# A two-block transformer kernel: order of the first modulation, packed attention scores and values, gates by pair, and fp32 one-hots in the expert selection

## The chip, the core and the metric

One core of a Trainium2 chip runs the whole program. The metric is the device time of one execution in microseconds (us), the median of several runs. The core has TensorE for matrix products (PE in the rows; PEld is its loading of the stationary operand), VectorE (DVE), ScalarE (ACT), GpSimd (POOL) and SyncE (SP, which issues most DMAs). Each engine takes its instructions in order.

## What is computed

One sequence of 512 tokens with 1024 features passes through two blocks. The first has two layers, retention and forgetting attention, each under a modulation by a vector `c`; the second has stick-breaking attention beside a gated delta rule, and then a layer that selects 16 experts for each token and head out of 16384. What matters here:

```python
c_act = jax.nn.silu(c)
shift, scale, gate = jnp.split(c_act @ mod_w[i] + mod_b[i], 3, axis=-1)
h = _rms_norm(x, norm_g[i]) * (1.0 + scale[:, None, :]) + shift[:, None, :]
...
# forgetting attention: 16 heads of 64, blocks of 128 query rows
logits = (jnp.einsum('bhqd,bhkd->bhqk', q[:, :, qs:qe], k[:, :, :qe])
          + cum[:, :, qs:qe, None] - cum[:, :, None, :qe])
p = jax.nn.softmax(jnp.where(causal, logits, -jnp.inf), axis=-1)
outs.append(jnp.einsum('bhqk,bhkd->bhqd', p, v[:, :, :qe]))
...
return (o.astype(h.dtype) * jax.nn.silu(g)) @ w_out
...
# expert selection
cand = (v1[..., :, None] + v2[..., None, :]).reshape(B, S, PEER_HEADS, PEER_TOPK * PEER_TOPK)
vals, c = lax.top_k(cand, PEER_TOPK)
expert = e1 * PEER_N_KEYS + e2
gate = jax.nn.softmax(vals, axis=-1)
```

The whole is held to float32 accuracy. The kernel gets it from TensorE by splitting each operand into a rounded part (type float32r, "hi") and the rest ("lo"), and by taking hi·hi + hi·lo + lo·hi: three matrix products where one is meant (`mm3`, L213 to L215).

## The kernel before

A tile framework schedules the program: it orders each engine's instructions by its own plan, so that work of later steps stands between the work of earlier ones, and adds the semaphores. Where the code wants an order, it adds a dependency by hand (`add_manual_dep`, without a semaphore).

**Weights.** `weights` loads a 512 KB block into `wraw` (SP's queue, L203), rounds it on ACT (`whi`, L206) and takes the rest on DVE (`wlo`, L207). Three buffers of each.

**The start (`retention`, first part).** x is loaded, then the 8 blocks of modulation part 1 (scale) into the space of `hTh` and `hTl`, and the 8 of part 0 (shift) into that of `vh`, `vl`, `yh`, `yl`. `mod_first` makes one part: of the blocks named in `direct` the product with c goes to TensorE directly (8 small products each, L630); the others are summed on DVE (L642, then L645 with a running sum in `wlo`), and the sum goes to TensorE with 8 small products. `mod_part` adds the bias (L595). Of part 1 the blocks 4 to 7 are direct, of part 0 the blocks 0 and 1. A small product leaves two records in the trace. L505 brings the norm's factor R, L728 multiplies x by it (8 times), L738 to L740 make the layer's input `hTh`, `hTl`, and `pair` (L553) multiplies it by the first two weight blocks.

**Forgetting attention (`fox`).** Eight pairs of heads. `part_a(p)` projects q and k of a pair, normalizes them (`normed`) and transposes them into a PSUM bank "norm"; `values(g)` makes the values of two pairs, `gates(g)` the gates of two pairs, all with the three products. `part_b(h, g)` makes the scores of two blocks of 128 rows, i = 2g and 2g + 1, with n = 128(i + 1) columns: q and k of one head are 64 rows of the pair's tiles, so that the three products (L213 to L215) have 64 rows; then `pick` adds the forget sums `ncr` (L915, 128 rows), and a bf16 product the mask (L916). DVE takes the maximum (L918), ACT the exponential, and the probabilities are rounded to `ph`, their rest to `pl` (L925), both transposed (L933, L940) into `pt`. `part_c` multiplies them by the values (L957): three products for each key block, with stationary operands of the hi or the lo of both heads of the pair, of which one head's 64 rows of the result are used; L970 multiplies them by the gate. Score banks "mx" are three, transposes have one bank "tr", the result one, "po".

**Expert selection (`peer`).** In the stretch that makes the gate table, 96 groups of 4 tokens each take four one-hot rows times the gate (L1660, DVE: a bf16 `iob` of 0 to 127 compared with one pointer scalar and multiplied by another, written as float32), one bf16 comparison (L1662), a copy on ACT (L1664), and 4 products on TensorE (L1641). Meanwhile weight blocks of the next step are split, with their lo part on GpSimd (`self.lo`, L207 on POOL).

Of the kernel before, what the change touches and what calls it, by code (L numbers as in the profile page):

```python
# [140 lines left out]
class Kern:  # L141
# [4 lines left out]
    def __init__(self, tc, ctx, A, out):  # L146
        self.tc, self.nc, self.A, self.out = tc, tc.nc, A, out
        self.cst = self.pool(ctx, "cst")
        self.wp = self.pool(ctx, "wp", 3)
        self.sm = self.pool(ctx, "sm", 2)  # L150
        self.run = (None, [], None)
        self.bk = {}
        self.bs = ExitStack()
        self.banks(self.bs, side="right", acc=2, norm=1)
        self.bg = None
        self.lo = tc.nc.vector
        self.pre = None
        self.mods = {}
# [39 lines left out]
    def weights(self, src, shape, raw=None):  # L198
        if self.bg is not None:
            self.bg = self.bg if next(self.bg, 0) is None else None  # L200
        if raw is None:
            raw = self.wp.tile([128, 1024], F32, name="wraw")
        self.nc.sync.dma_start(raw, src)  # L203
        hi = self.wp.tile([128, 1024], F32R, name="whi")
        lo = self.wp.tile([128, 1024], F32R, name="wlo")
        self.nc.scalar.activation(hi, raw, AF.Copy)  # L206
# [54 lines left out]
    def normed(self, pool, ps, d, gains, out):  # L261
# [19 lines left out]
        for w in range(2):  # L281
            ps = self.ps("norm", (128, 4, 128))
            for t in range(4):
                nc.tensor.transpose(ps[:, t], raws[t // 2][:, t % 2, 128 * w:128 * w + 128], self.ident)
            hi, lo = out[w]
            p2 = ps.rearrange("p a b -> p (a b)")
            nc.scalar.activation(hi, p2, AF.Copy, scale=gains[:, w:w + 1])
            nc.vector.scalar_tensor_tensor(lo, p2, gains[:, w:w + 1], hi.bitcast(F32), op0=OP.mult, op1=OP.subtract)
# [28 lines left out]
    def narrow(self, pool, tag, src):  # L317

        nc = self.nc
        fr = pool.tile([128, 8, 16], F32, name="fr")  # L320
        nc.sync.dma_start(fr, src)
        fh = pool.tile([128, 8, 16], F32R, name="fh")
        fl = pool.tile([128, 8, 16], F32R, name="fl")
# [267 lines left out]
    def mod_part(self, part, ps, md, bias, g, a1):  # L591
# [3 lines left out]
        nc.vector.tensor_add(md[:, s], ps[:, :, 0], bias[:, s])  # L595
# [23 lines left out]
    def mod_first(self, part, ws, acc, tag, tiles, direct):  # L619
# [17 lines left out]
        begun = False  # L637
        for k in range(8):
# [5 lines left out]
            else:  # L644
                nc.vector.scalar_tensor_tensor(acc, ws[k], self.cact[:, k:k + 1], acc, op0=OP.mult, op1=OP.add)  # L645
            yield
        products(acc, self.ones2, True)
        self.mod_part(part, ps, *tiles)
# [39 lines left out]
    def retention(self):  # L688
        nc, A = self.nc, self.A
        off = (0, 512, 896, 1152)  # L690
        with ExitStack() as cx:
# [25 lines left out]
            v = small[:, 0:4]  # L717
            nc.vector.tensor_scalar(v, ss[:, :, 0], 1.0 / D, EPS, op0=OP.mult, op1=OP.add)
# [14 lines left out]
            self.pre = [self.weights(A["ret_qk"][0, i], (8, 128)) for i in range(2)]  # L733
            mod = self.mod(0, mp, "norm", tiles, (2,))
            self.hT = [self.cst.tile([128, 8, T], F32R, name=n) for n in ("hTh", "hTl")]
            for k in range(8):
                hi, lo = self.hT[0][:, k], self.hT[1][:, k]
                nc.scalar.activation(hi, ts[k], AF.Identity, bias=b0[:, k:k + 1], scale=a0[:, k:k + 1])  # L738
                nc.vector.tensor_scalar(ts[k], ts[k], a0[:, k:k + 1], b0[:, k:k + 1], op0=OP.mult, op1=OP.add)
                nc.vector.tensor_sub(lo, ts[k], hi.bitcast(F32))  # L740
            QK, V, PR, SG, Y = {}, {}, {}, {}, {}
# [100 lines left out]
    def fox(self):  # L842
# [3 lines left out]
        with ExitStack() as cx:  # L846
            self.banks(cx, mx=3, tr=1, po=1)
# [4 lines left out]
            ncr = self.rows_pair(pool, "ncr", 1)[0]  # L852
            ncum = pool.tile([128, 4, 16], F32, name="ncum")

            def forget():
# [11 lines left out]
                ones = pool.tile([128, 8, 16], F32, name="fr").rearrange("p a b -> p (a b)")  # L867
# [9 lines left out]
                self.split_rows(ncr, ps, 16)  # L877
# [3 lines left out]
            def part_a(p):  # L881

                ps = self.pair_wide() if self.pre else self.proj_wide(A["fox_qk"][p], self.hT)
                for w in range(2):
                    QK[p, w] = [pool.tile([128, T], F32R, name=f"qk{w}" + "hl"[z], bufs=2) for z in range(2)]
                self.normed(pool, ps, 64, gains, [QK[p, w] for w in range(2)])

            def values(g):

                pv = self.proj_wide(A["fox_v"][g], self.hT)  # L890
                for a in range(2):
                    v = V[2 * g + a] = [pool.tile([128, 4, 128], F32R, name="fv" + "hl"[z], bufs=3) for z in range(2)]
                    for t in range(2):
                        ts = slice(2 * t, 2 * t + 2)
                        self.split(v[0][:, ts], v[1][:, ts], pv[t][:, :, a * 128:a * 128 + 128])

            def gates(g):
                sg = SG[g] = pool.tile([128, 2, T], F32, name="fsg")
                for m in range(2):
                    pg = self.proj_cols(A["fox_g"][2 * g + m], self.hT)  # L900
                    self.act(sg[:, m], pg, AF.Silu)

            def part_b(h, g):

                p, e = divmod(h, 2)
                (qh, ql), (kh, kl) = QK[p, 0], QK[p, 1]
                r = slice(64 * e, 64 * e + 64)
                pt = PT[h, g] = pool.tile([128, 2, 4, 256], F32R, name="pt", bufs=2)
                for i in (2 * g, 2 * g + 1):
                    n = 128 * (i + 1)  # L910
                    s = slice(i * 128, n)
                    ps = self.ps("mx")
# [31 lines left out]
            def part_c(h, g):  # L944
# [7 lines left out]
                for j in range(2 * g + 2):  # L952
                    c = 128 if j == 2 * g + 1 else 0
                    for a, b in ((0, 0), (0, 1), (1, 0)):


                        m = mm(PO[h][:, 256 * g + c:256 * g + 256], v[a][:, j], pt[:, b, j, c:],  # L957
                               start=first is None and g == 0, stop=j == 2 * g + 1 and a == 1, skip_group_check=True).ins
# [7 lines left out]
                if g == 1:  # L966
                    if e == 0:
                        YP[p] = pool.tile([128, T], F32, name="yp")
                    r = slice(64 * e, 64 * e + 64)
# [10 lines left out]
            gates(0)  # L980
            for p in range(8):
                if p < 7:
                    part_a(p + 1)
                for e in range(2):
# [5 lines left out]
                if p % 2 == 1 and p < 7:  # L990
                    gates(p // 2 + 1)
# [10 lines left out]
            ss, add = self.sums("mx", g, g2, pool.tile([128, T], F32, name="sqg"))  # L1002
# [484 lines left out]
    def peer(self):  # L1487
# [5 lines left out]
        with ExitStack() as cx:  # L1493
# [12 lines left out]
            iob = tp.tile([128, 128], BF, name="iob")  # L1506
            nc.vector.tensor_copy(iob, io)
# [146 lines left out]
            for g in range(96):  # L1654
# [131 lines left out]
```

## Time and profile before

| | before |
|---|---|
| median of 3 runs | 3068.15 us (3055.47, 3068.15, 3070.58) |
| the profiled execution | 3056.85 us, of which the span of instructions is 3055.1 us |
| PE busy | 2916.9 us (95%), PEld 2536.2 us |
| DVE, ACT, POOL busy | 2133.6 us (70%), 1309.9 us (43%), 697.4 us (23%) |
| chain that ended last | PE 72%, DVE 14%, issue 4%, ACT 4%, POOL 4%, DMA 2% |
| DMA | 516.67 MB, 169 GB/s over the span |

The program runs through its stages once: start (0 to 54 us), retention (to about 516), forgetting attention (to about 935), stick-breaking attention, delta rule, merge (to about 1712), expert selection (to about 2080) and the experts (to the end). TensorE is busy nearly throughout; a busy engine is not one at its peak, since the record of a product lasts longer than the step from its start to the start of the next one. The step is what a product costs a full engine, and it is read from the starts of successive rows.

### The profile page before, as it was taken

To read this page: it belongs to the slowest core of one execution; us is meant where nothing else is said; L and a number is where in the kernel's file an instruction comes from. 1 tells how busy PE (TensorE), PEld (TensorE's weight loads), DVE (VectorE), ACT (ScalarE), POOL (GpSimd) and SP (SyncE) were. 2 spreads that over 40 slices of the span, in tenths; PEclk is the share of its full clock that TensorE was granted. 3 is DMA by queue.
4 is the path that set the end of the run, shared out by engine and by line. 5 is a ranking of instruction groups with operands and counts; after the bars stand their busy time and mean duration, and the time that the engine had idled before them with its cause. 6 is when DMAs were issued, how large, how long until landed. Compare 5 with 4: busy or idle time off the path is not lost.

```text
span 3055.1 us, 44135 instructions
## 1 busy us (share of the span) xinstructions
PE 2916.9 (95%) x16816; PEld 2536.2 (83%) x16820; DVE 2133.6 (70%) x4130; ACT 1309.9 (43%) x2275; POOL 697.4 (23%) x524
## 2 busy tenths in 40 slices
PE   6999999999999999999898999989999999999999
PEld 5887887888879897777787887888899999999977
DVE  5576457455565645698866687995877778888885
ACT  2222234455455534577245334774333333333333
POOL 0111011000001000012003354213555554333350
PEclk9999999999999999999999999999999999999999
DMA  5343221111212132434445232667988888888773
GB/s 213 132 167 123 90 83 66 61 49 49 70 54 93 42 111 98 156 124 156 134 155 190 75 105 84 182 185 265 345 304 297 297 295 302 301 300 308 280 288 135
DMA packets 201011, 516.67 MB, mean 169 GB/s; under 512 B 27104, under 2 KB 79456, under 8 KB 198496
## 3 DMA queue, kind: packets, MB, share of 16 engines
q1 hardware_dynamic: 163504, 379.36, 36.1%
q0 software_dynamic: 36864, 134.23, 12.0%
q8 instruction: 132, 2.16, 0.3%
q14 instruction: 79, 0.65, 0.1%
q10 hardware_dynamic: 432, 0.27, 0.0%
HBM read 462.15 MB, written 51.64 MB: 168 GB/s over the span
## 4 chain that ended last, share of the span: by engine, by line
PE 72%; DVE 14%; issue 4%; ACT 4%; POOL 4%; DMA 2%; SPq 0%; ACTq 0%; POOLq 0%; DVEq 0%
PE pacc L213 10%; PE pacc L214 9%; PE pacc L215 9%; PE pst L215 5%; PE pst L214 5%; PE pst L213 5%; PE out L214 5%; PE out L215 5%; PE out L213 5%; DVE t L1660 3%; POOL g L1707 2%; DVE wlo L207 1%; PE ppo L957 1%; DVE cv L1217 1%; ACT whi L206 1%
## 5 line engine op out<-in xcount | busy, mean ns | idle before, releaser
L206 ACT ACTIVATE whi<-wraw 128x1024 fp32r<-128x1024 f32 x346 | 364.0, 1054 | 494.8 <-PE pacc L214 225.8
L207 DVE TENSOR_TENSOR wlo<-wraw,whi 128x1024 fp32r<-128x1024 f32 x299 | 375.9, 1258 | 252.7 <-ACT whi L206 251.3
L215 PE MATMUL pst<-hTh,wlo 128*128 128x384 f32 x1024 | 349.3, 341 | 0.6 <-DVE wlo L207 0.6
L213 PE MATMUL pst<-hTh,whi 128*128 128x384 f32 x1024 | 348.0, 340 | 1.0 <-ACT whi L206 1.0
L214 PE MATMUL pst<-hTl,whi 128*128 128x384 f32 x1024 | 347.1, 339 | 0.0
L213 PE MATMUL pacc<-whi,hTh 128*128 128x256 f32 x1216 | 341.1, 281 | 3.4 <-ACT whi L206 1.6
L214 PE MATMUL pacc<-wlo,hTh 128*128 128x256 f32 x1216 | 340.1, 280 | 0.0
L215 PE MATMUL pacc<-whi,hTl 128*128 128x256 f32 x1216 | 339.2, 279 | 0.0
L214 PE MATMUL out<-wlo,wh 128*128 128x512 f32 x768 | 304.1, 396 | 5.3 <-DVE wlo L207 5.3
L215 PE MATMUL out<-whi,wl 128*128 128x512 f32 x768 | 303.4, 395 | 1.2 <-DVE wl L191 1.2
L213 PE MATMUL out<-whi,wh 128*128 128x512 f32 x768 | 303.2, 395 | 1.2 <-ACT wh L190 1.2
L1707 POOL DMA_INDIRECT g<-in_peer_u_dram,ex x128 | 226.6, 1771 | 211.1 <-DVE w L1733 187.1
L206 ACT ACTIVATE whi<-vr 128x1024 fp32r<-128x1024 f32 x126 | 133.5, 1059 | 279.3 <-PE pst L214 239.2
L1707 POOL DMA_INDIRECT g<-in_peer_v_dram,ex x128 | 176.2, 1376 | 255.4 <-DVE w L1733 231.0
L213 PEld LDWEIGHTS pacc<-whi,hTh 128*128 128x128 f32 x1216 | 229.0, 188 | 5.2 <-ACT whi L206 1.8
L215 PEld LDWEIGHTS pacc<-whi,hTl 128*128 128x128 f32 x1216 | 229.3, 189 | 0.4
L214 PEld LDWEIGHTS pacc<-wlo,hTh 128*128 128x128 f32 x1216 | 228.9, 188 | 0.5
L213 PE MATMUL pacc<-hTh,whi 128*128 128x512 f32 x560 | 222.5, 397 | 2.0 <-DVE old L1103 1.5
L215 PE MATMUL pacc<-hTh,wlo 128*128 128x512 f32 x560 | 222.1, 397 | 0.1
L214 PE MATMUL pacc<-hTl,whi 128*128 128x512 f32 x560 | 222.1, 397 | 0.0
L190 ACT ACTIVATE wh<-w 128x384 fp32r<-128x384 f32 x128 | 67.1, 524 | 330.0 <-PE out L214 264.5
L213 PEld LDWEIGHTS pst<-hTh,whi 128*128 128x128 f32 x1024 | 192.6, 188 | 7.4 <-ACT whi L206 1.3
(648 smaller groups left out, 6819.3 us busy)
## 6 DMA issues: line engine op xcount, KB each, us to landing
wraw<-in_peer_ut_dram SPq DMA_DIRECT2D x128, 512.0 KB
vr<-in_peer_v_dram SPq DMA_DIRECT2D x126, 512.0 KB
gd<-big SPq DMA_DIRECT2D x24, 1024.0 KB
gg<-gd SPq DMA_DIRECT2D x16, 1536.0 KB
wraw<-in_mod_w_dram SPq DMA_DIRECT2D x32, 512.0 KB
wraw<-in_ret_vg_dram SPq DMA_DIRECT2D x32, 512.0 KB
wraw<-in_gdn_qkv_dram SPq DMA_DIRECT2D x24, 512.0 KB
gd<-pk SPq DMA_DIRECT2D x8, 1280.0 KB
```

The lines of the kernel that those rows point to most:

```text
L190: nc.scalar.activation(hi, src, AF.Copy)
L206: self.nc.scalar.activation(hi, raw, AF.Copy)
L207: self.lo.tensor_tensor(lo, raw, hi.bitcast(F32), op=OP.subtract)
L213: first = mm(ps, lh, rh, start=start, stop=False, **kw)
L214: mm(ps, lh, rl, start=False, stop=False, **kw)
L215: mm(ps, ll, rh, start=False, stop=stop, **kw)
L957: m = mm(PO[h][:, 256 * g + c:256 * g + 256], v[a][:, j], pt[:, b, j, c:], start=first is None and g == 0, stop=j == 2 * g + 1 and a == 1, ...
L1217: nc.vector.scalar_tensor_tensor(cv, x[:, i:i + T], cw[:, w, h, i:i + 1], cv, op0=OP.mult, op1=OP.add)
L1660: nc.vector.tensor_scalar(o1[:, i], iob, eg[0][:, n:n + 1], gtT[:, n:n + 1], op0=OP.is_equal, op1=OP.mult)
L1707: i = nc.gpsimd.indirect_dma_start(out=g, out_offset=None, in_=A["peer_u" if up else "peer_v"], in_offset=bass.IndirectOffsetOnAxis(ap=ex[ ...
```

## The change

**Start.** Part 1 has only the blocks 6 and 7 direct, part 0 only block 0; the other sums are DVE's. The order is set by hand: R and the 8 products by R first, then both sums, and both parts' final steps behind; the split of the first two weight blocks is placed ahead of the last bias step, and the products that make `hTh` and `hTl` behind that split. `consts` moves behind them.

**Scores.** For each head of a pair and each of the two pair parities there are tiles of 128 rows: `q1` holds q's hi in the head's 64 rows and q's lo in the other 64; `k1` holds k's hi in both. One product of 128 rows gives hi·hi + lo·hi. `S2` holds q's hi and, in the other half, the selector of the head; `M2` holds k's lo and the forget sums: a second product gives hi·lo and the forget term. The halves are written by ACT and DVE (with 64 instead of 128 partitions, twice as many) and by copies on GpSimd: q's hi, k's hi and the selector, two of each for a pair, and four memsets once. The forget sums are split into four tiles instead of one.

**Values.** A head's stationary operand holds the hi and the lo of its values side by side. Two products (with `ph` and `pl`) for each key block replace three; ACT copies one half of the result out of PSUM, DVE adds the other half, and the gate is multiplied on GpSimd once for a pair.

**Banks and order.** Transposes of q and k use "tr", which has two banks; scores use two banks "mx" and the bank "norm" in turn. `pt` has one buffer for each g. Gates are made for one pair, ahead of its scores. `narrow` takes buffers of the name "raw".

**Expert selection.** The one-hot rows are made from the float32 `io`; `iob` is gone.

```diff
@@ class Kern, weights
-        self.lo.tensor_tensor(lo, raw, hi.bitcast(F32), op=OP.subtract)
+        j = self.lo.tensor_tensor(lo, raw, hi.bitcast(F32), op=OP.subtract)
+        self.parts = (i.ins.name, j.ins.name)
@@ normed
-            ps = self.ps("norm", (128, 4, 128))
+            ps = self.ps(tag, (128, 4, 128))
...
+            if callable(out):
+                out(w, p2)
+                continue
@@ mod_part
-        nc.vector.tensor_add(md[:, s], ps[:, :, 0], bias[:, s])
+        i = nc.vector.tensor_add(md[:, s], ps[:, :, 0], bias[:, s])
+        if self.late:
+            self.tc.add_manual_dep(i.ins, self.late, ..., reason="order")
@@ retention
-            m1 = self.mod_first(1, slots[:8], self.wp.tile([128, 1024], F32, name="wlo"), "norm", tiles, (4, 5, 6, 7))
-            for _ in m1:
-                pass
...
-            m0 = self.mod_first(0, slots[8:], self.wp.tile([128, 1024], F32, name="wlo"), "qk", tiles, (0, 1))
-            for _ in m0:
-                pass
-            self.consts()
+            for _ in range(8):
+                next(m1)
+            m0 = self.mod_first(0, slots[8:], self.wp.tile([128, 1024], F32, name="wlo"), "qk", tiles, (0,))
+            for _ in range(8):
+                self.late = next(m0) or self.late
+            for _ in range(2):
+                next(m1)
+            self.late = None
             self.pre = [self.weights(A["ret_qk"][0, i], (8, 128)) for i in range(2)]
+            self.late = self.parts[1]
+            for _ in range(2):
+                next(m0)
...
+                self.tc.add_manual_dep(i.ins, self.parts[0], nosync, reason="order")
+                self.tc.add_manual_dep(j.ins, self.parts[1], nosync, reason="order")
                 nc.vector.tensor_sub(lo, ts[k], hi.bitcast(F32))
+            self.consts()
@@ fox
-            self.banks(cx, mx=3, tr=1, po=1)
+            self.banks(cx, mx=2, tr=2, po=1)
...
+            S2 = [[pool.tile([128, T], F32R, name=f"sq{e}{b}") for b in range(2)] for e in range(2)]
+            M2 = [[pool.tile([128, T], F32R, name=f"mk{e}{b}") for b in range(2)] for e in range(2)]
+            for e in range(2):
+                for b in range(2):
+                    nc.gpsimd.memset(M2[e][b][HALF[1 - e]].bitcast(F32), 0.0)
...
+                    nc.gpsimd.tensor_copy(S2[e][p % 2][HALF[1 - e]],
+                                          self.sel[0:64, 2 * p + e].to_broadcast([64, T]))
+                def parts(w, x):
+                    for e in range(2):
+                        r, o = HALF[e], HALF[1 - e]
+                        g = gains[r, w:w + 1]
+                        t = QK[p, e][w]
+                        nc.scalar.activation(t[r], x[r], AF.Copy, scale=g)
+                        if w == 0:
+                            nc.vector.scalar_tensor_tensor(t[o], x[r], g, t[r].bitcast(F32), op0=OP.mult, op1=OP.subtract)
+                            nc.gpsimd.tensor_copy(S2[e][p % 2][r], t[r])
+                        else:
+                            nc.gpsimd.tensor_copy(t[o], t[r])
+                            nc.vector.scalar_tensor_tensor(M2[e][p % 2][r], x[r], g, t[r].bitcast(F32),
+                                                           op0=OP.mult, op1=OP.subtract)
...
-                    self.mm3(ps[:, :n], qh[r, s], ql[r, s], kh[r, :n], kl[r, :n], True, False)
-                    mm(ps[:, :n], self.pick(h), ncr[:, :n], start=False, stop=False)
+                    mm(ps[:, :n], q1[:, s], k1[:, :n], start=True, stop=False)
+                    mm(ps[:, :n], q2[:, s], k2[:, :n], start=False, stop=False)
                     mm(ps[:, s], self.identb, self.m_gt, start=False, stop=True)
...
-                    for a, b in ((0, 0), (0, 1), (1, 0)):
-                        m = mm(PO[h][:, 256 * g + c:256 * g + 256], v[a][:, j], pt[:, b, j, c:],
+                    for b in range(2):
+                        m = mm(PO[h][:, 256 * g + c:256 * g + 256], v[:, j, 2 * e:2 * e + 2].rearrange("p a b -> p (a b)"), pt[:, b, j, c:],
...
-                    nc.vector.tensor_mul(YP[p][r], PO[h][r], SG[p // 2][r, p % 2])
+                    y = YP[p][r]
+                    nc.scalar.activation(y, PO[h][o], AF.Copy)
+                    nc.vector.tensor_add(y, y, PO[h][r])
                     if e:
+                        nc.gpsimd.tensor_tensor(YP[p], YP[p], SG[p], op=OP.mult)
@@ peer
-                    nc.vector.tensor_scalar(o1[:, i], iob, eg[0][:, n:n + 1], gtT[:, n:n + 1], op0=OP.is_equal, op1=OP.mult)
+                    nc.vector.tensor_scalar(o1[:, i], io, eg[0][:, n:n + 1], gtT[:, n:n + 1], op0=OP.is_equal, op1=OP.mult)
```

Where the instructions stand, first on TensorE at the start of the program, before (`ones_81` and `cact_79` are constants made of c, `pnorm` and `pqk` PSUM banks):

```order
L714 MATMUL pqk<-ones_81,sqa 128x2 x4
L503 MATMUL pnorm<-ident,ao 128x128 x4
L630 MATMUL pnorm<-cact_79,hTl 128x2 x32
L630 MATMUL pnorm<-ones_81,wlo 128x2 x8
L630 MATMUL pqk<-cact_79,vh 128x2 x16
L630 MATMUL pqk<-ones_81,wlo 128x2 x8
```

and after:

```order
L723 MATMUL pqk<-ones_81,sqa 128x2 x4
L508 MATMUL pnorm<-ident,ao 128x128 x4
L638 MATMUL pnorm<-cact_79,hTl 128x2 x16
L638 MATMUL pnorm<-ones_81,wlo 128x2 x6
L638 MATMUL pqk<-cact_79,vh 128x2 x8
L638 MATMUL pnorm<-ones_81,wlo 128x2 x2
L638 MATMUL pqk<-ones_81,wlo 128x2 x8
```

Of 64 small products 40 are left; nothing else moved ahead of them.

On TensorE in the middle of forgetting attention, two score blocks before (`qk1h`, `qk0h` are hi of k and of q, `ncr` the forget sums):

```order
L213 MATMUL pmx<-qk1h,qk0h 128x256
L214 MATMUL pmx<-qk1l,qk0h 128x256
L215 MATMUL pmx<-qk1h,qk0l 128x256
L915 MATMUL pmx<-ncr_4633,k_sel 128x256
L916 LDWEIGHTS identb
L916 MATMUL pmx<-m_gt,identb 128x128
L213 MATMUL pmx<-qk1h,qk0h 128x384
L214 MATMUL pmx<-qk1l,qk0h 128x384
L215 MATMUL pmx<-qk1h,qk0l 128x384
L915 MATMUL pmx<-ncr_4633,k_sel 128x384
```

and after (`k`, `q` are the packed tiles, `mk` is `M2`, `sq` is `S2`; `ptr` is a transpose bank):

```order
L286 MATMUL ptr<-ident,raw 128x128 x4
L964 MATMUL pnorm<-k_5601,q_5600 128x256
L286 MATMUL ptr<-ident,raw 128x128 x4
L965 MATMUL pnorm<-mk_4616,sq_4612 128x256
L966 LDWEIGHTS identb
L966 MATMUL pnorm<-m_gt,identb 128x128
L964 MATMUL pmx<-k_5601,q_5600 128x384
L965 MATMUL pmx<-mk_4616,sq_4612 128x384
L966 LDWEIGHTS identb
L966 MATMUL pmx<-m_gt,identb 128x128
```

Four long products of a block have become two, all of 128 rows, and the banks alternate.

On GpSimd where retention hands over to forgetting attention, before (`rsy` is a power that the second half's norm waits for, `xh` a product for the next layer's input):

```order
L343 TENSOR_TENSOR rsy<-rsv_4515,nhalf 128x2
L517 TENSOR_TENSOR xh<-xT,R 128x256 x2
L343 TENSOR_TENSOR rsy<-rsv_4564,nhalf 128x2
L517 TENSOR_TENSOR xh<-xT,R 128x256 x6
L478 TENSOR_TENSOR sqg<-sqg,xh 128x256 x6
```

and after:

```order
L348 TENSOR_TENSOR rsy<-rsv_4494,nhalf 128x2
L879 MEMSET mk_4616 64x512
L879 MEMSET mk_4617 64x512
L879 MEMSET mk_4618 64x512
L879 MEMSET mk_4619 64x512
L918 COPY sq_4612<-k_sel 64x512
L918 COPY sq_4614<-k_sel 64x512
L522 TENSOR_TENSOR xh<-xT,R 128x256 x2
L918 COPY sq_4613<-k_sel 64x512
L918 COPY sq_4615<-k_sel 64x512
L522 TENSOR_TENSOR xh<-xT,R 128x256
L348 TENSOR_TENSOR rsy<-rsv_4543,nhalf 128x2
```

The second `rsy` stands behind two more copies and one more product.

## Rows read from the trace of the kernel before

**Rows 1.** Busy us by stretch: PE, PEld, DVE, ACT, POOL (instructions), PEclk, DMA share, GB/s
```profile
0.00:54.00 54.00, 31.57 (x144) 31.02 (x144) 26.63 (x53) 9.54 (x16) 2.15 (x5) 1.00 0.67 252
550.00:905.00 355.00, 351.98 (x2322) 294.54 (x2320) 200.28 (x414) 178.63 (x380) 2.36 (x4) 0.99 0.16 55
935.00:1905.00 970.00, 919.52 (x5235) 771.75 (x5239) 674.67 (x1777) 466.48 (x880) 171.79 (x163) 0.99 0.35 118
1905.00:2080.00 175.00, 160.49 (x1117) 148.31 (x1116) 161.07 (x481) 132.27 (x234) 35.12 (x15) 1.00 0.63 184
```

**Rows 2.** Timeline of the start: start us, us, engine, line, operation, names, shape, count
```profile
24.71 13.81 PE L630 MATMUL pnorm<-cact,hTl 128*128 128x2 f32 x64 [0.69 <-ACT R L505]
28.31 1.29 DVE L728 TENSOR_TENSOR kl<-xT,R 128x512 f32<-128x512 f32 x2
...
42.26 0.75 DVE L642 TENSOR_SCALAR wlo<-vl,cact 128x1024 f32<-128x1024 f32 x1
...
47.00 2.61 DVE L645 SCALAR_TENSOR_TENSOR wlo<-yl,cact,wlo 128x1024 f32<-128x1024 f32 x2
...
49.66 3.57 PE L630 MATMUL pqk<-ones,wlo 128*128 128x2 f32 x16 [0.90 <-DVE wlo L645]
...
55.97 1.23 DVE L207 TENSOR_TENSOR wlo<-wraw,whi 128x1024 fp32r<-128x1024 f32 x1
...
64.60 0.69 DVE L740 TENSOR_TENSOR hTl<-kl,hTh 128x512 fp32r<-128x512 f32 x1
...
71.20 2.00 ACT L206 ACTIVATE whi<-wraw 128x1024 fp32r<-128x1024 f32 x2 [9.14 <-PE pqk L553]
```

**Rows 3.** DMA rate from 0 to 60 us in 40 slices of 1.5 us
```profile
GB/s 0 147 322 253 313 405 407 410 412 407 410 410 401 366 407 415 410 404 412 403 378 391 325 415 393 60 0 0 0 0 5 0 0 0 0 0 0 0 41 306
```

**Rows 4.** Timeline of PE, one score block of 512 columns
```profile
866.46 0.23 PE L916 MATMUL pmx<-m_gt,identb 128*128 128x128 bf16 x1
866.50 0.43 PE L940 MATMUL ptr<-identr,pl 128*128 128x128 f32 x3
866.86 0.50 PE L213 MATMUL pmx<-qk1h,qk0h 64*128 64x512 f32 x1
867.20 0.39 PE L214 MATMUL pmx<-qk1l,qk0h 64*128 64x512 f32 x1
867.43 0.39 PE L215 MATMUL pmx<-qk1h,qk0l 64*128 64x512 f32 x1
867.75 0.50 PE L915 MATMUL pmx<-ncr,k_sel 128*128 128x512 f32 x1
868.10 0.23 PE L916 MATMUL pmx<-m_gt,identb 128*128 128x128 bf16 x1
868.25 0.32 PE L213 MATMUL pmx<-qk1h,qk0h 64*128 64x128 f32 x1
```

**Rows 5.** Timeline of PE, products of probabilities and values
```profile
589.28 0.40 PE L957 MATMUL ppo<-pt,fvh 128*128 128x256 f32 x2
589.52 0.28 PE L957 MATMUL ppo<-pt,fvl 128*128 128x256 f32 x1
589.64 0.40 PE L957 MATMUL ppo<-pt,fvh 128*128 128x256 f32 x2
```

**Rows 6.** POOL's forms: shapes, count | busy us, mean ns | idle before
```profile
L1592 POOL COPY gate<-gt 128x128 f32<-128x128 f32 x1 | 0.4, 421 | 3.6 <-DVE gt L1591 3.6
```

**Rows 7.** Timeline: POOL at the hand-over, and later beside the one-hot rows
```profile
515.24 0.87 POOL L343 TENSOR_TENSOR rsy<-rsv,nhalf 128x2 f32<-128x2 f32 x1 [0.83 <-DVE rsv L494]
...
2018.20 2.46 POOL L207 TENSOR_TENSOR wlo<-wraw,whi 128x1024 fp32r<-128x1024 f32 x1 [10.28 <-ACT whi L206]
```

**Rows 8.** DVE's one-hot rows (min/median/max ns), and two TENSOR_SCALAR rows of the start
```profile
L1660 DVE TENSOR_SCALAR t<-iob,eg,gtT x384: 328/336/2466, 1891.9 to 2076.7; 128x128 f32<-128x128 bf16 x192
7.46 0.49 DVE L657 TENSOR_SCALAR ra<-rb,inv 128x512 f32<-128x512 f32 x1 [1.08 <-DMA inv<-in_k_inv_dram]
54.32 0.55 DVE L739 TENSOR_SCALAR qh<-qh,A,mod 128x512 f32<-128x512 f32 x1 [0.88 <-ACT hTh L738]
```

More of the change, by code (lines that the diff above doesn't have):

```diff
@@ L259, in pair_wide, with normed @@
         return ps
-    def normed(self, pool, ps, d, gains, out):
+    def normed(self, pool, ps, d, gains, out, tag="norm"):
         nc = self.nc
@@ L319, in narrow @@
         nc = self.nc
-        fr = pool.tile([128, 8, 16], F32, name="fr")
+        fr = pool.tile([128, 2, 256], F32, name="raw", bufs=3)[:, 0, :128].rearrange("p (a b) -> p a b", a=8)
+        fhl = pool.tile([128, 2, 256], F32R, name="raw", bufs=3)
+        fh, fl = [fhl[:, i, :128].rearrange("p (a b) -> p a b", a=8) for i in range(2)]
         nc.sync.dma_start(fr, src)
-        fh = pool.tile([128, 8, 16], F32R, name="fh")
-        fl = pool.tile([128, 8, 16], F32R, name="fl")
         self.split(fh, fl, fr)
@@ L594, in mod_part @@
         s = slice(8 * part, 8 * part + 8)
-        nc.vector.tensor_add(md[:, s], ps[:, :, 0], bias[:, s])
+        i = nc.vector.tensor_add(md[:, s], ps[:, :, 0], bias[:, s])
+        if self.late:
+            self.tc.add_manual_dep(i.ins, self.late, mybir.DependencyInfo(mybir.DependencyClass.NoSync, mybir.DependencyReason.DATA),
+                                   reason="order")
         if part == 1:
@@ L635, in products @@
                     first.append(i.name)
-        begun = False
+        begun, last = False, None
         for k in range(8):
@@ L644, in mod_first @@
             else:
-                nc.vector.scalar_tensor_tensor(acc, ws[k], self.cact[:, k:k + 1], acc, op0=OP.mult, op1=OP.add)
-            yield
+                last = nc.vector.scalar_tensor_tensor(acc, ws[k], self.cact[:, k:k + 1], acc, op0=OP.mult, op1=OP.add)
+            yield begun and last and last.ins.name
         products(acc, self.ones2, True)
+        yield
         self.mod_part(part, ps, *tiles)
@@ L891, in values, with gates @@
                 for a in range(2):
-                    v = V[2 * g + a] = [pool.tile([128, 4, 128], F32R, name="fv" + "hl"[z], bufs=3) for z in range(2)]
+                    v = V[2 * g + a] = pool.tile([128, 4, 4, 64], F32R, name="fv", bufs=3)
                     for t in range(2):
                         ts = slice(2 * t, 2 * t + 2)
[L895 to L901, printed above, removed]
+                        self.split(v[:, ts, 0::3], v[:, ts, 1:3],
+                                   pv[t][:, :, a * 128:a * 128 + 128].rearrange("p t (e d) -> p t e d", e=2))
+            def gates(p):
+                sg = SG[p] = pool.tile([128, T], F32, name="fsg", bufs=2)
+                self.act(sg, self.proj_cols(A["fox_g"][p], self.hT), AF.Silu)
             def part_b(h, g):
                 p, e = divmod(h, 2)
-                (qh, ql), (kh, kl) = QK[p, 0], QK[p, 1]
-                r = slice(64 * e, 64 * e + 64)
-                pt = PT[h, g] = pool.tile([128, 2, 4, 256], F32R, name="pt", bufs=2)
+                (q1, k1), q2, k2 = QK[p, e], S2[e][p % 2], M2[e][p % 2]
+                pt = PT[h, g] = pool.tile([128, 2, 2 * g + 2, 256], F32R, name=f"pt{g}")
                 for i in (2 * g, 2 * g + 1):
@@ L953, in part_c @@
                     c = 128 if j == 2 * g + 1 else 0
-                    for a, b in ((0, 0), (0, 1), (1, 0)):
-                        m = mm(PO[h][:, 256 * g + c:256 * g + 256], v[a][:, j], pt[:, b, j, c:],
-                               start=first is None and g == 0, stop=j == 2 * g + 1 and a == 1, skip_group_check=True).ins
+                    for b in range(2):
+                        m = mm(PO[h][:, 256 * g + c:256 * g + 256], v[:, j, 2 * e:2 * e + 2].rearrange("p a b -> p (a b)"), pt[:, b, j, c:],
+                               start=first is None and g == 0, stop=j == 2 * g + 1 and b == 1, skip_group_check=True).ins
                         if first is None:
@@ L979, in fox @@
             values(0)
-            gates(0)
             for p in range(8):
@@ L983, in fox @@
                     part_a(p + 1)
+                gates(p)
                 for e in range(2):
```

38 lines of the change are left out of this document (21 added, 17 removed).

## The prediction, made before the changed kernel ran

> **What bounds the kernel now.** I began with the shares of busy time on the page, which only say that TensorE is the fullest engine. Then the stretches [rows 1]: in forgetting attention, 550 to 905 us, PE is busy 351.98 of 355.00 us, with DVE at 200.28, ACT at 178.63 and GpSimd (POOL) at 2.36; so that stretch ends when PE has done its work, and what shortens PE's steps there shortens the program, as long as the other engines keep up. The gate table, 1905 to 2080, has PE at 160.49 and DVE at 161.07 of 175.00: two engines nearly full, so a change of DVE's rows there may show. The start, 0 to 54, has PE at 31.57 of 54, and needs a look at its own rows. Last I read the timelines: the starts of successive rows give the step, which is what a product costs a full PE.
>
> **The start.** PE's 64 records of small products take 13.81 us from 24.71 [rows 2], 0.216 us each. By the code there are 128 such records before (64 products), and the last 16, behind the DVE sum L645, stand at 49.66 and end at 53.23 [rows 2]. Behind them L739 waits for the modulation. After the change 80 records are left, 80 × 0.216 = 17.3 us from 24.7, so PE could be free at 42. DVE then has: R near 24.7, 8 products by R (L728, 0.645 us each) to 29.9, one remaining step of sum 1 (1.3) to 31.2, sum 0 of one L642 (0.75) and six L645 (2.61 / 2 = 1.3 each), together 8.6, to 39.8, then 16 records at 0.216, 3.5, to 43.3. That is 53.2 − 43.3 = 9.9 us earlier. The data must be there: the transfers run at about 410 GB/s until about 37.5 us and then stop [rows 3]; that last stretch also carries the weights behind the modulation blocks, about 2.5 MB or 6 us, so the last block lands near 31, ahead of its sum step. Two L207 (1.23 each, the one at 55.97 is shown) leave the stretch in which L738 to L740 make the layer's input, which now ends at 64.60 with L740 [rows 2]: they move into DVE's wait for the small products, worth up to 2.5 more, of which PE's first pair (which holds ACT's next split until 71.20 [rows 2]) returns about half. I take **−11 us**; the bounds are −6 (the last block lands late) and −13.
>
> **The scores.** A block of 512 columns is read from its starts [rows 4]: L213 at 866.86, L214 0.34 later, L215 0.23 after that, L915 0.32, L916 0.35, and the next block 0.15 after L916: 1.39 us. The bare rate is L214's, 0.23 / 512 = 0.45 ns a column; all other steps hold something more, at each change between 64 and 128 rows. L916 in front of 128-row transposes costs 0.04 (866.46 to 866.50 [rows 4]) instead of 0.15. After the change all rows are 128: 0.23 + 0.35 + 0.04 = 0.62, so 0.77 is saved. The mean block has 320 columns, and two of four streams go: 0.77 − 2 × 192 × 0.45 ns = 0.60 us. There are 16 heads × 4 = 64 blocks: 38 us, and a little where a transpose ahead of a block pays for the change of rows as well (64 × 0.11 = 7 at most). I take **−40**. Floor: only the two streams go, 2 × 320 × 0.45 ns × 64 = 18. Ceiling 47.
>
> **The values.** Three L957 of 256 columns start 0.36 us apart in all (589.28 to 589.64 [rows 5]), 0.12 each. Of 288 such products (16 heads × 18; a third of them with 128 columns) 96 go. Two thirds at 0.12 and one third near 0.1 give **−11**; bounds −6 and −13.
>
> **What forgetting attention gives back.** PE's demand falls to 352 − 51 = 301. DVE gets 16 more halves of splits of 512 columns, at 0.69 like L740 [rows 2] 11 us: 211. The sum that replaces the product by the gate is one row for one row. ACT gets 16 gains and 16 copies out of PSUM, at most 1 us each by L206 (2.00 for two of 1024 columns [rows 2]): under 211. POOL gets about 60 instructions: a copy of 128 columns is 0.421 [rows 6], a two-source one of 1024 is 2.46 [rows 7]; those here have 512 columns on 64 partitions, so between 0.42 and 1.23, I take 0.8: 48 us. Even if each held DVE for its length, DVE would be at 259 of 301. So all are covered, but PE is no longer alone: the stretch 935 to 1905, where DVE is busy 674.67 of 970 (70%), has PE idle in 5% [rows 1], against 1% here now. With DVE at 70% (211 of 301) I take that: 5% of 301 is 15, less the 3 us idle already there, gives 12; POOL's longer chain (a copy behind each gain, 0.8 us) acts the same way, while the two transpose banks and the gates for one pair spread the work. I take **+8**, bounds +3 and +15.
>
> **The hand-over.** The second `rsy` (L343, at 515.24 [rows 7]) now stands behind two copies and one more product on POOL. Behind it wait DVE's norm of the half, and PE's next layer. Two copies at 0.8 and a product near 0.6 are 2.2; the memsets come before, where POOL has idle time. I take **+2**, bounds 0 and +4.
>
> **The one-hot rows.** L1660 takes 336 ns in the median, with a bf16 source and a float32 destination, 128 columns [rows 8]. A float32 one: L657 is 0.49 for 512 columns, L642 0.75 for 1024 [rows 2, 8], a slope of 0.26 / 512 = 0.51 ns a column; L739 with two pointers is 0.55 for 512, so 0.55 − 384 × 0.51 ns = 0.354 for 128. 384 rows at 0 to 18 ns more are 0 to 7 us, in a stretch where DVE is near full. The median is near the float32 estimate already: I take **+2**.
>
> The other stages keep their work; the buffers of `narrow` shift the order by a few rows, for which I put 0 ± 2.
>
> **Sum.** −11 − 40 − 11 + 8 + 2 + 2 = −50. Against the profiled execution's 3056.85 that is 3007; against the median of 3068.15, 3018. Two of the three runs are near the latter, one near the former: I forecast the middle, **3012 us**. With every term at its low end (−13, −47, −13, +3, 0, 0, and −2 for the order) it is −72 and 2985 from the profiled time. The forecast's own range is about 2986 to 3028.
>
> **The rivals.**
> *A: the stretch becomes bound by its chain.* Scores, maximum, exponential, rounding, transposes, values and the bank's release follow one another, and DVE, ACT and now POOL are in it; PE's shorter steps then only lengthen its waits, and two thirds of the 51 us come back, 33 in place of 8. For it: PE now covers all of that with 352 us and would have 301. Against it: two blocks and the next pair's projection stand between. 3012 + 25 = 3037. Chance 0.15.
> *B: the change of rows is not what the long steps pay for.* If the 0.35 of L915 and its like remain whatever the rows, only the two dropped streams are saved, 18 instead of 40: 3034. For it: L915 has 128 rows and still costs 0.12 more than the bare 0.23. Chance 0.08.
> *D: the source's type sets the rate of a one-hot row.* Then the column part of a float32 row, 128 × 0.51 = 65 ns, was half as long with bf16, and 33 ns × 384 = 13 us come on a full DVE, 11 more than taken: 3023. Against it: 336 ns is what float32 rows extrapolate to, and the destination is float32 in both. Chance 0.04. The Trainium skill has a rule for it (VectorE: DVE Perf Modes, section "The perf-mode tier table (the rule you actually need)"): `tensor_scalar` gets the 4× mode with bf16 in SBUF and only 2× with fp32. By that rule the edit would cost time in this stage; the row above does not bear out that the mixed-type row was in the faster mode.
> *C, slower than before: POOL's copies hold DVE.* One L1660 lasts 2466 ns where the median is 336 [rows 8], and POOL's L207 at 2018.20 lasts 2.46 us [rows 7]: a DVE row can stand still for a whole POOL instruction. Place: the 60 new POOL instructions of forgetting attention. DVE has 211 + 60·x; it passes the 355 us of now at x = 2.4 us, and the whole program becomes slower at x = 2.5, since the start still gives its 11. At x = 3 the stretch takes 391, +36 − 11 + 4 = +29: 3086 to 3097, about 3092. Against it: a copy of 128 columns is 0.421, and even four times that is 1.7. Chance 0.05. The Trainium skill says of it (SBUF — State Buffer, section "SBUF: two separate sides") that VectorE and GpSimd share a port pair as an exclusive lock, held for the whole instruction. By that rule, which speaks against moving copies to GpSimd, the trace's 2466 ns agrees.
>
> **How the numbers follow.** Forecast 0.68, A 0.15, B 0.08, C 0.05, D 0.04. A and B lie inside 3040 for the most part, so the range is 2986 to 3040. A measurement of this kernel can tell about 0.5% from no change, 15 us: faster is below 3052.8. C makes 0.04 of slower and 0.01 of same; 0.02 of same come from A with a worse return. Faster 0.93, same 0.03, slower 0.04.
>
> **What would show it.** Start: 80 records of small products, the last ending near 43 instead of 53; if the sums of DVE wait for a transfer, that step is wrong. Scores: at 512 columns, steps of 0.23, 0.35 and 0.04; a block step near 1 us speaks for B. Values: 192 products at 0.12. Forgetting attention: the stretch about 310 us, PE's idle time in it between 3 and 15 us; over 30 is A. POOL: 64-partition copies with a mean under 1.2 us; over 2.4 with DVE rows as long beside them is C. One-hots: a median of 336 to 354 ns; 370 is D. The forecast is wrong as a whole if PE's busy time falls and the span does not.

## The result, and the profile after

The changed kernel takes 3006.71 us (median of 4 runs, 3004.63 to 3013.39) where the kernel before takes 3065.98 beside it: ratio 0.9821, 95% interval 0.9805 to 0.9836. Two later comparisons of the same pair gave 0.9833 (0.982 to 0.9847) and 0.9823 (0.9805 to 0.9841). The forecast was 3012 in a range of 2986 to 3040, and faster; the line that it set for faster was 3052.8.

| | after |
|---|---|
| the profiled execution | 3007.45 us, span 3005.6 us (before: 3055.1) |
| PE busy | 2859.3 us (95%) |
| DVE, ACT, POOL busy | 2159.1, 1340.1, 747.0 us |

The stretches of after that answer to [rows 1], with the same columns:

```profile
0.00:44.00 44.00, 21.33 (x96) 20.78 (x96) 32.55 (x58) 11.37 (x18) 2.15 (x5) 1.00 0.83 311
540.00:850.00 310.00, 297.27 (x2086) 261.21 (x2085) 219.81 (x432) 208.18 (x424) 38.68 (x53) 1.00 0.19 62
880.00:1854.00 974.00, 922.49 (x5218) 775.66 (x5217) 672.74 (x1773) 464.47 (x877) 170.99 (x162) 0.99 0.35 117
1854.00:2032.00 178.00, 162.76 (x1126) 149.60 (x1125) 163.38 (x484) 133.57 (x237) 36.73 (x15) 1.00 0.62 181
```

Forgetting attention fell from 355 to 310 us, and the start from 54 to 44. PE is no longer alone there: 297.27 of 310 busy, 4% idle, against 1%. The two last stretches, cut at the same work, became longer by 4 and 3 us.

Where the time went is best seen by an anchor: the same product in both traces, and the difference of its start. It is +0.4 at the first small product, −11.5 at the first product of `pair`, −15.3 at 140 us and −15.6 at the end of retention, −56.3 at the last product of the layer that follows forgetting attention's output (881 us in after), −55.7 at the first stick-breaking score, −51.0 at the last product of the stick-breaking scores (1162 us), −50.4 at the end of the merge, −47.8 at the end of the gate table and −49.5 at the last product. In the table, the rows "other differences" and "the rest" are what is left over between these anchors:

| stretch | predicted | measured |
|---|---|---|
| start, with what follows from it in retention | −11 (−13 to −6) | −15.3 |
| scores, steps summed over all blocks, without PE's idle time | −40 (−47 to −18) | 68.1 to 29.7: −38.4 |
| values, steps summed in the same way | −11 (−13 to −6) | 36.2 to 23.4: −12.8 |
| PE idle in forgetting attention and the hand-over | +8 and +2 | 11.7 to 23.1: +11.4 |
| other differences of that stage | 0 | −1.2 |
| stick-breaking attention | 0 ± 2 | +4.7 |
| gate table with the one-hot rows | +2 (0 to 7) | +2.6 |
| the rest | 0 | −0.5 |

Start, the rows of the timeline of after that answer to [rows 2]:

```profile
25.11 6.99 PE L638 MATMUL pnorm<-cact,hTl 128*128 128x2 f32 x32 [0.69 <-ACT R L510]
...
37.17 2.61 DVE L653 SCALAR_TENSOR_TENSOR wlo<-yl,cact,wlo 128x1024 f32<-128x1024 f32 x2
...
39.83 3.58 PE L638 MATMUL pqk<-ones,wlo 128*128 128x2 f32 x16 [0.91 <-DVE wlo L653]
...
43.45 0.17 DVE L600 TENSOR_TENSOR mod<-pqk,modb 128x8 f32<-128x8 f32 x1 [0.85 <-PE pqk L638]
...
44.51 0.80 PE L558 MATMUL pqk<-hTh,whi 128*128 128x256 f32 x2 [1.11 <-ACT hTh L754]
```

The small products end at 43.41 (forecast 43.3), DVE's sums wait for no transfer, and `pair` starts 1.1 us behind them instead of 2.8.

A score block of 512 columns and one of 128 behind it, on PE, to be read against [rows 4], and seven products with the values, against [rows 5]:

```profile
604.07 0.48 PE L964 MATMUL pnorm<-k,q 128*128 128x512 f32 x1
604.39 0.40 PE L965 MATMUL pnorm<-mk,sq 128*128 128x512 f32 x1
604.63 0.23 PE L966 MATMUL pnorm<-m_gt,identb 128*128 128x128 bf16 x1
604.67 0.31 PE L964 MATMUL pmx<-k,q 128*128 128x128 f32 x1
604.81 0.27 PE L965 MATMUL pmx<-mk,sq 128*128 128x128 f32 x1
604.93 0.23 PE L966 MATMUL pmx<-m_gt,identb 128*128 128x128 bf16 x1
...
569.40 0.93 PE L1007 MATMUL ppo<-pt,fv 128*128 128x256 f32 x7
570.17 0.25 PE L983 MATMUL ptr<-identr,pl 128*128 128x128 f32 x1
```

The block takes 604.67 − 604.07 = 0.60 us, where 0.62 was forecast and 1.39 stood before; but it is the first product that costs more than the bare 0.23 (0.32), not the second (0.24). The seven products take 0.77, 0.11 each.

GpSimd's forms in forgetting attention (columns as in [rows 6]), and the one-hot rows (as in [rows 8]):

```profile
L1024 POOL TENSOR_TENSOR yp<-yp,fsg 128x512 f32<-128x512 f32 x8 | 10.3, 1287 | 102.1 <-DVE yp L1022 102.1
L930 POOL CAST sq<-q 64x512 fp32r<-64x512 f32 x14 | 8.9, 633 | 138.0 <-ACT q L926 137.9
L933 POOL CAST k<-k 64x512 fp32r<-64x512 f32 x14 | 8.6, 612 | 0.8
L918 POOL CAST sq<-k_sel 64x512 fp32r<-64x512 f32 x12 | 7.3, 611 | 36.6 <-PE pmx L965 16.9 <-PE pnorm L965 11.1 <-PE pmx L966 7.6
```
```profile
L1709 DVE TENSOR_SCALAR t<-io,eg,gtT x384: 328/334/2482, 1843.0 to 2028.8; 128x128 f32<-128x128 f32 x192
```

A copy is 0.61 to 0.63 us (0.8 was taken), and a float32 one-hot row 334 ns in the median against 336.

### The profile page after: what moved, and what is told of

It is laid out like the page before. It is cut to its first block, busy times and chain, and to the rows that moved or that the text cites. A ratio compares the mean times of both kernels' runs of the same rounds, so it can differ in the third digit from the quotient of the medians.

```text
span 3005.6 us, 43767 instructions
## 1 busy us (share of the span) xinstructions
PE 2859.3 (95%) x16548; PEld 2502.3 (83%) x16548; DVE 2159.1 (72%) x4151; ACT 1340.1 (45%) x2317; POOL 747.0 (25%) x584
## 4 chain that ended last, share of the span: by engine, by line
PE 67%; DVE 15%; ACT 6%; issue 6%; DMA 3%; POOL 3%; SPq 0%; POOLq 0%; DVEq 0%; ACTq 0%
PE pacc L215 8%; PE pacc L216 8%; PE pacc L217 8%; PE pst L217 5%; PE pst L216 5%; PE pst L215 5%; PE out L216 5%; PE out L215 5%; PE out L217 5%; DVE t L1709 2%; DVE wlo L208 2%; ACT whi L207 1%; POOL g L1756 1%; DVE cv L1268 1%; ACT L181 1%
```

## Experiments

Every one is an edit of the changed kernel. e2 to e4 are compared with e1, and f2 to f4 with f1, the changed kernel run beside them; e5 to e8 have no such run beside them and are compared with its 3006.71 and with the stretches of its first trace.

**e1, f1: the changed kernel again.**

> The changed kernel once more, as the base of the other three runs. If the half-speed stretches of TensorE that its first profile shows at 500.4 (6.8 us), 998.8 (3.4 us) and 1821.4 (3.4 us) belong to the order of its work, they stand at the same places again; if the grant of the clock is chance, they have moved. Time 3004 to 3013 us either way.

> The changed kernel as the base of the other three. Its half-speed stretches stand at the same places as in its first two profiles (500, 860, 999, 1457, 1593, 1665, 1822, 2064 us), with lengths that differ by multiples of 3.4 us: 3006 to 3013.

3009.6 (3008.65 to 3014.16) and 3008.65 us (3006.82 to 3013.41). Most half-speed stretches stand in the same places of the program, but not all: the one at 1821.4 us stands in e1 and not in f1, and one at 360 us in f1 alone. So the place belongs to the work, and whether and how long the clock falls there is not fixed.

**e5: the old start.** The blocks 4 to 7 and 0, 1 are direct again, in the old order:

```diff
-            m1 = self.mod_first(1, ..., (6, 7))
+            m1 = self.mod_first(1, ..., (4, 5, 6, 7))
...
-            m0 = self.mod_first(0, ..., (0,))
+            m0 = self.mod_first(0, ..., (0, 1))
```

> The changed kernel with the start of the kernel before (blocks 4 to 7 and 0, 1 direct, the old order, consts ahead of the layer's input). Theory: the new start is worth the whole shift that the traces show by 140 us, 15.3 us (11.5 at the first product of pair, the rest behind it): about 3022. Rival: the 3.8 us behind the first product come from elsewhere, and only 11 to 12 come back: 3018.

3028.72 us (3027.63 to 3033.26). By the anchors the loss is 11.5 us at the first product of `pair`, 14.7 at 139 us and 14.6 at the end of retention: so 3.1 of the 3.8 us behind the first product belong to the start, as the theory had it, and 0.7 do not come back. Of them, 1.7 arise at 76 us, where before ran at half clock for 3.4 us (75.4), e5 too (76.3), and after not; the others are waits in the first projections, of which before has more (4.7 us in 73 to 140, after 2.3). In the whole time the edit costs more than either expectation, 19 to 22 us; 4 of that arise at the end of forgetting attention, where its half-speed stretch is 13.7 us long instead of 6.8.

**e6: two more products of 128 rows in each score block**, with a tile of zeros:

```diff
                     mm(ps[:, :n], q2[:, s], k2[:, :n], ...)
+                    mm(ps[:, :n], q1[:, s], zk[:, :n], ...)
+                    mm(ps[:, :n], q2[:, s], zk[:, :n], ...)
```

> Each score block of the changed kernel takes two more products of 128 rows with a tile of zeros, so that four long products stand in it again, all of 128 rows. Theory (the change between 64 and 128 rows cost the old blocks more than the dropped products did): 2 x 320 columns x 0.45 ns x 64 blocks = 18 us, so the score products' steps go from 29.7 us to 48 and not to the 68.1 of before: about 3025. Rival B (the products themselves cost that much): to 68, 38 us more: 3045. A third way: PE's idle time of 11 us in this stage takes some of it: 3017.

3026.94 us (3023.41 to 3031.05); the stage grows by 19.5 us between its first and last mask product. The timeline of PE of this kernel, one block:

```profile
613.86 0.40 PE L965 MATMUL pmx<-mk,sq 128*128 128x512 f32 x1
...
614.15 0.45 PE L965 MATMUL pmx<-zk,q 128*128 128x512 f32 x1
614.44 0.40 PE L965 MATMUL pmx<-zk,sq 128*128 128x512 f32 x1
```

The steps of the 128 products sum to 24.4 us, those of the whole score blocks to 53.3: four streams, as in the old blocks, cost 53 here and 68 in the old blocks. So 24 us of the saving were the products, and 15 the rest in which the two blocks differ; rival B, which gave that rest nothing, falls. That it is the change of rows is argued and not isolated, since e6 also keeps the new banks and neighbours. The theory's split (18 and 20) was off mainly because the extra products of 128 columns step at 0.20 us in the mean (0.11 to 0.29) and not at 128 × 0.45 ns = 0.06: 4.4 of the 6 us.

**e7: the copies on GpSimd twice.**

```diff
+                            nc.gpsimd.tensor_copy(S2[e][p % 2][r], t[r])
...
+                            nc.gpsimd.tensor_copy(t[o], t[r])
```

> Each copy of q's and of k's hi on GpSimd in forgetting attention is made twice, 32 more copies of 0.62 us: 20 us more of GpSimd. Theory: GpSimd is off the path and holds up no one for its length; PE's idle time in the stage stays under 15 us and the time within 4 us: 3007 to 3011. Rival (GpSimd's copies hold DVE, or stand in the chain that PE waits for): at least half of the 20 us shows: 3017 or more.

3012.48 us (3009.58 to 3014.0). The time is 1.5 us above what was expected and far from the rival's 3017. From the first to the last mask product the stage grows by 3.6 us for 20 us more of GpSimd; in its middle (543 to 846 us) PE's idle time is 11.5 us against 11.2. GpSimd's copies are hidden for the most part, and with twice as many of them the kernel is still 53 us faster than the kernel before beside it (3065.29).

**e8: bf16 one-hots**, with `iob` made again.

```diff
-   nc.vector.tensor_scalar(o1[:, i], io, eg[0][:, n:n + 1], ...)
+   nc.vector.tensor_scalar(o1[:, i], iob, eg[0][:, n:n + 1], ...)
```

> The one-hot rows of the changed kernel are made from the bf16 tile again. Theory: the rows take 336 ns from either type (334 was the median with float32), the time stays within 1 us: 3006 to 3008. Rival: the 1.0 us by which the stretch with the rows became longer, or more, is theirs: 3004 to 3006.

The row of this kernel, by type and duration:

```profile
L1709 DVE TENSOR_SCALAR t<-iob,eg,gtT x384: 328/335/2454, 1843.9 to 2029.7; 128x128 f32<-128x128 bf16 x192
```

335 against 334 ns: the type costs nothing, and the stretch with the rows is as long as in after (anchors +0.9 and +0.9). The time, 3012.39 (3009.65 to 3020.75), spreads too far to say more.

**e3: the selector copies behind the power.**

```diff
+                    p < 2 and self.tc.add_manual_dep(j.ins, pw, ..., reason="order")
```

> The first four selector copies on GpSimd stand behind the second power rsy by a dependency. Theory: the copies ahead of it delay rsy by 2.06 us (501.90 against 515.24 - 15.4), and PE waits 1.32 and 0.72 us around it and then runs at half speed for 6.8 us instead of 3.4: 2 to 4 us less, about 3004. Rival: PE waits there for DVE's hTl whatever rsy does: under 1 us, 3006.5.

The hand-over on after, then on e3:

```profile
500.87 0.58 PE L254 MATMUL pacc<-whi,hTl 128*128 128x256 f32 x1 [1.32 <-DVE hTl L531]
...
501.90 0.70 POOL L348 TENSOR_TENSOR rsy<-rsv,nhalf 128x2 f32<-128x2 f32 x1
...
503.24 0.58 PE L254 MATMUL pacc<-whi,hTl 128*128 128x256 f32 x1 [0.72 <-DVE hTl L531]
```
```profile
501.59 0.87 POOL L348 TENSOR_TENSOR rsy<-rsv,nhalf 128x2 f32<-128x2 f32 x1 [1.61 <-DVE rsv L499]
...
501.96 0.58 PE L254 MATMUL pacc<-whi,hTl 128*128 128x256 f32 x1 [0.41 <-DVE hTl L531]
```

The waits of 1.32 and 0.72 become one of 0.41, but by the anchors only 0.9 us is gained by 523 us: the half-speed stretch of 6.8 us stays. In e3 it starts at 498.7 us, ahead of the wait for `hTl` and where PE waits 2.7 us for `sqa`, as it does in after (2.9) and before (2.7); so it comes without the waits that the edit took away. Both expectations missed the size: under 1 us, but through rsy. The time is no better, 3014.92 (3004.51 to 3015.44); in the profiled run the clock is at half for 20.5 us at the end of forgetting attention:

```profile
853.70:874.20 20.50, 18.66 (x85) 18.05 (x85) 11.56 (x29) 9.43 (x23) 5.51 (x7) 0.50 0.39 136
```

The same length stands there in e4 and f2, and 6.8 to 13.7 us in the others; whether the edits had a part in it is open.

**e2, f3: `narrow` with buffers of its own in the second block.**

```diff
-        fr = pool.tile([128, 2, 256], F32, name="raw", bufs=3)...
-        fhl = pool.tile([128, 2, 256], F32R, name="raw", bufs=3)
+        fr = pool.tile([128, 8, 16], F32, name="fr") if tag == "acc" else ...
+        fhl = pool.tile([128, 2, 128], F32R, name="fhl") if tag == "acc" else ...
```

> In the second block, narrow takes buffers of its own again instead of the three that normed uses. Theory: with the shared buffers the 16-column products of narrow could not start early, so PE had nothing to do while it waited for sp3h (1.92 us, and 2.6 us in all up to 1018) and ran at half speed for 3.4 us behind that; with its own buffers these products stand in that gap again. The stretch from 985 to 1069 us of the old kernel then takes 84 us again instead of 88.7: 4.7 us less, about 3002. Rival: the order of work there is no cause and the clock's drop is chance: no change, 3007.

> The kernel of e2 once more. Theory: 4 to 6 us less than the base of this call, as the first time. Rival: the first time's difference was that of the granted clock in those runs: less than 2 us.

PE of before, of after, then of e2, at the same place (`sp3h` is a part of the stick-breaking sums; the rows with `fl`, `raw` and `fhl` are `narrow`'s):

```profile
1052.43 0.40 PE L215 MATMUL pacc<-hTh,fl 128*16 128x512 f32 x1
1052.69 0.33 PE L1084 MATMUL pz<-sp3h,ntri 128*128 128x128 f32 x1
```
```profile
994.96 0.23 PE L1123 MATMUL pz<-m_le,identb 128*128 128x128 bf16 x1
...
997.11 0.33 PE L1135 MATMUL pz<-sp3h,ntri 128*128 128x128 f32 x1 [1.92 <-DVE sp3h L1130]
...
1004.07 0.40 PE L215 MATMUL pacc<-hTh,raw 128*16 128x512 f32 x1
```
```profile
999.15 0.40 PE L215 MATMUL pacc<-hTh,fhl 128*16 128x512 f32 x1
999.38 0.39 PE L216 MATMUL pacc<-hTl,fhl 128*16 128x512 f32 x1
999.61 0.40 PE L217 MATMUL pacc<-hTh,fhl 128*16 128x512 f32 x1
999.87 0.33 PE L1135 MATMUL pz<-sp3h,ntri 128*128 128x128 f32 x1
```

In before nine products of `narrow` stood ahead of `sp3h`'s; in after the first of them starts 7 us behind it; in e2 nine fill the wait again. And the clock, in windows of after (the third column from the end is the granted clock):

```profile
995.00:998.80 3.80, 1.69 (x10) 1.12 (x9) 3.76 (x15) 3.80 (x14) 0.00 (x0) 1.00 0.40 138
998.80:1002.20 3.40, 3.40 (x17) 3.32 (x18) 2.79 (x9) 1.77 (x4) 0.00 (x0) 0.50 0.00 0
```

All nine profiles without this edit have a half-speed stretch there (998.7 to 1018.4 us), the four with it (e2, f3, e4, f4) have none. Between the first and the last product of the stick-breaking scores (929 to 1162 us in after), e2 is 4.0 us shorter than after's first profile, f3 3.9, e4 4.8, f4 5.1; the kernels without the edit lie between 0 and 1.3 us shorter. The whole times are 3003.84 (3001.88 to 3007.15; ratio 0.981, 0.9797 to 0.9823) against e1's 3009.6, and 3008.68 (3001.58 to 3015.9; 0.9806, 0.9788 to 0.9825) against f1's 3008.65. The second pair does not bear out 4 to 6 us in the median; the profiled run of f3 loses 9.4 us near 2900, where PE waits 7.5 us for `wl` and DVE 8.9 us for a gather of `peer_v`. Over ten runs each the means are 3005.9 and 3010.2.

**e4, f2, f4: both edits; the last pair's gate on DVE; that with e2's edit.**

```diff
-                        nc.gpsimd.tensor_tensor(YP[p], YP[p], SG[p], op=OP.mult)
+                        (nc.vector if p == 7 else nc.gpsimd).tensor_tensor(YP[p], YP[p], SG[p], op=OP.mult)
```

> The two edits before together. Theory: the two stretches lie 500 us apart and share nothing, so the gains add: 6 to 9 us less than the changed kernel, about 2999. Rival: what one stretch gains is lost again at a later wait: under 3 us, 3004 or more.

> The product of the last pair by its gate is made on DVE instead of GpSimd. In the changed kernel the last ppo goes through ACT (837.94), DVE and GpSimd (1.28 us) to ACT's split at 840.65, 2.71 us, where the old kernel took 0.73 from 895.77 to 896.50. Theory: this chain is what PE waits for at the end of the stage (0.51 us before the product by fyh, and what follows); DVE's 0.69 for 1.28 gives back 0.6 us of it, within 1 us of the base. Rival: a shorter idle time of PE there also spares a half-speed stretch of 3.4 us and more: 2 to 4 us less.

> Both edits: 5 to 7 us less than the base, about 3003, and within 2 us of f3.

e4: 3015.66 (3002.47 to 3020.75). Its two stretches gain 0.8 and 4.8 us, about as they do alone, and 4.5 us are lost at the end of forgetting attention and 9.4 near 2900. So the gains add in the trace and do not show in the time. f2: 3010.17 (3007.18 to 3014.75), 1.5 us above f1; the 0.6 us of the theory can't be seen in that, and the rival's 2 to 4 us less do not show. In the trace PE's wait of 0.5 us for `fyh` becomes 0.3 for `fyh` and 0.3 for `fyl`, so nothing is gained there. f4: 3006.3 (3004.86 to 3010.02), 2.4 us less than f1 where 5 to 7 were expected.

No edit gives a kernel that is clear of the changed one in the whole time of a single comparison; e2's is the best by mean. No run takes back the values, the banks or the order of the gates alone.

## Why the prediction was right, and where it was not

**The start** was right in its mechanism and its chain (43.41 against 43.3), and its term mis-sized: −15.3, outside −13. The step that failed is the end of the sum at the first product of `pair`: the edit also moved DVE's and ACT's work out of the next projections, where before lost 4.7 us in waits (after 2.3) and 1.7 to a half-speed stretch, and I had priced nothing behind `pair`.

**Scores and values** hold: −38.4 and −12.8 against −40 and −11. The block's sum was right (0.60 against 0.62) with its parts in other places. The prediction put what a long step holds at a change of rows, but the 0.35 behind L915 has 128 rows on both sides, and in after it is the first product of a block that is long. By e6 the dropped streams are 24 us and not 18, and the rest 15 and not 20: B falls, and that the term came out at its size is partly luck, two errors of opposite sign.

**The give-back** holds: +11.4 against 8 and 2. A is not what happened. The waits of PE from 500 to 880 us in after, the largest five (waiting engine, operation, line, then what ended the wait: us in all, times, longest):

```profile
PE ptr L286 <- DVE raw L282: 4.5, 6, 1.4
PE pacc L254 <- DVE hTl L531: 2.8, 4, 1.3
PE pacc L254 <- ACT hTh L191: 2.2, 2, 1.7
PE pacc L215 <- DVE xT L541: 2.1, 4, 1.1
PE pacc L215 <- DVE fv L192: 2.1, 5, 0.6
```

They are spread: q and k's norm on DVE (`raw`) now comes late for its transposes, 4.5 us, and nothing holds PE for long. The clock is not what came back: from the hand-over to 937 us (881 in after) PE ran at half speed for 17.1 us in before and 13.7 in after. Taking the share from another stage with DVE at 70% gave the right size; DVE is busy 71% here (219.81 of 310), but no run shows that DVE's share sets it.

**The hand-over** was +2: rsy starts 501.90 against 515.24 − 15.4, 2.06 us late, as worked out, but only half of it by GpSimd's queue. The `rsv` that it needs was itself 1.1 us late on DVE; its row in after, then in before:

```profile
500.74 0.14 DVE L499 TENSOR_SCALAR rsv<-pqk 128x2 f32<-128x2 f32 x1
```
```profile
515.01 0.15 DVE L494 TENSOR_SCALAR rsv<-pqk 128x2 f32<-128x2 f32 x1
```

Of the 2.06 us e3 brings back 0.9 by 523 us; the term was a bit too large, and the half-speed stretch there (6.8 us, 3.4 before) was not in it.

**C and D** fall: copies of 0.61 to 0.63 us, and e7's 20 us more cost 3.6; 334 against 335 ns for the two types. The one-hots are 0 and not +2; the gate table's +2.6 is in part the clock: 1.5 us of it arise at 1821.4, behind the same waits of 1.2 and 1.8 us that before has. The other 1.0 arises beside the one-hot rows and stays with bf16 (e8); its cause is open. Windows of after:

```profile
1818.00:1821.40 3.40, 1.59 (x9) 0.86 (x8) 3.32 (x4) 2.27 (x6) 1.81 (x1) 1.00 0.13 40
1821.40:1824.80 3.40, 3.39 (x13) 3.39 (x14) 1.28 (x2) 1.85 (x3) 0.00 (x0) 0.50 0.28 114
```

and of before:

```profile
1868.00:1871.40 3.40, 1.90 (x11) 1.23 (x12) 3.37 (x4) 2.65 (x6) 2.19 (x1) 1.00 0.08 18
1871.40:1874.80 3.40, 3.01 (x21) 2.74 (x21) 1.62 (x3) 2.27 (x5) 0.00 (x0) 1.00 0.37 136
```

In the third column from the end, the granted clock is 0.50 (1.2 GHz) in the one and 1.00 (2.4 GHz) in the other.

**"The other stages keep their work, 0 ± 2"** failed: +4.7 in stick-breaking attention. The sentence took a shared buffer as a shift of a few rows; it took from the scheduler what filled a wait. e2 shows it in its place.

**The sum**, −50 from one profile to the other, met −49.5, but partly by luck: the start was 4 too small, stick-breaking 5 too large, with opposite signs. Between the medians the change is worth more, 52 to 59 us; the profiled execution of before was one of its quickest (3056.85 in 3055.47 to 3070.58), with a mean granted clock of 0.994, where the runs of before in these comparisons have 0.987 to 0.993. Putting the forecast between the two origins was what left it 5 us above the result.

## What to carry to other kernels

When PE is full, price a product by the step from its start to the next start, by size and by what stands on either side, and sum over all; here that gave 51 us of 104 (scores and values) before the run, and 51 were measured, though the parts of a block were not where they had been put. When a change lets two steps share buffers, look for which of them PE used as filler while it waited for another engine, since a wait of 2 us there was paid twice, once as idle time and once in clock. An edit of 1 to 5 us is judged in its own stretch between two anchors, because single waits and half-speed stretches move the whole time of one and the same kernel by 4 to 18 us.

## What the runs showed of the hardware

TensorE's granted clock falls to 0.50 for 3.4 us and more in or behind stretches in which PE waited (500.4, 998.8, 1821.4 in after), at nearly the same places of the program in each run, but not in every run: the same waits at 1868 in before, and at the same place in f1, left it at 1.00. Within the span it was at half speed for 34.1 us in before's profile and 47.8 in after's; half of that, 17 and 24 us, is the clock that was lost. A GpSimd copy of 64 partitions and 512 columns took 0.61 to 0.63 us, against 0.421 for 128 columns on 128 partitions.
